# Two-layer attention encoder: the norms between the layers and the transposed rows, ScalarE and VectorE put in the order in which they are written

## The chip, the cores and the metric

The kernel runs on one core of one Trainium2 chip. The metric is the device time of one execution in microseconds (us), less is better. A trace holds one execution as the hardware profiler saw it; its span runs from the first instruction to the last, and the time of that execution is a little longer.

## What is computed

A token sequence of 512 rows of width 1024 goes through two layers in float32. Layer A is latent attention, layer B differential attention whose keys and values come from one projection of the residual stream. The part between them is what the change touches:

```
def rmsnorm(x, g):
    y = x * rsqrt(mean(x * x) + EPS)
    return y * g
# end of layer A
o = (o * silu(z)) @ a_w_o
h = x + rmsnorm(o, a_post_g)          # first norm of a token tile
# start of layer B
u  = rmsnorm(h, b_kv_norm_g)          # second norm of a token tile
k, v = split(u @ b_w_kv)              # kb and vb in the kernel
u2 = rmsnorm(h, b_pre_g)              # same norm, other gain
q, z = split(u2 @ b_w_in)             # qb and zb
```

## The kernel before

The 512 tokens are four tiles of 128 rows, called tile 0 to tile 3 here. Every product in float32 is made of three TensorE matmuls over a high and a low part of each operand (`mm3`, lines 186 to 188): for operands w and x these are high·high, then two mixed ones. So each operand is first split: a copy that rounds to the high part (ScalarE by default, line 130, or GpSimd, line 132) and a subtraction that gives the low part (VectorE, line 135).

At the end of layer A, `wo_end` multiplies the gated attention output (`ogh`, `ogl`) by the output weights. Each tile has two halves of 512 columns in PSUM: `st["acc"]` and `st["o1"]`, both called wo in the trace. After a tile's last matmul `done_a(i)` is called. It runs `chain_a(i)`, the two norms of the tile: two squares with a sum on ScalarE (`sq<-wo`), the product with the gain on VectorE (line 633), v (the mean square, line 620), Ln and Exp on ScalarE (lines 304, 305: a first 1/sqrt), a Newton step on VectorE (lines 307 to 309), the new residual rows (`xr`, line 635), and then the same once more for the second norm (`rh`) over `xr`. Last, the first half of the normed rows is written to `hTf` by ScalarE (line 728) and the second half by GpSimd (line 726), which also stores `xr` to DRAM.

These normed rows have their tokens on the partitions. The next products want the tokens along the free dimension, so TensorE transposes them: `trans_h(i)`, eight transposes into two PSUM banks (`hT`). `evac_h(i)` takes them out: a copy on ScalarE (line 747), the product with the gain on VectorE (`hg`, line 749), and the split into `hT1h` (ScalarE) and `hT1l` (VectorE). Within `done_a(2)` TensorE transposes tile 0, within `done_a(3)` tile 1; tiles 2 and 3 are transposed in `vb_half0`, behind the products vb of tile 0 and of tile 1.

`vb_half0` makes the first half of layer B's values, one tile after the other (vb, 24 matmuls each: four pairs of contraction blocks, of which blocks 0 to 3 need the first half of `hT1h` and `hT1l` of that tile, blocks 4 to 7 the second half). Each is taken out by a split into `vhb` and `vlb`. Behind it the units of the key projection follow, kb, each 24 matmuls with a weight of its own.

The weights come through a stream of units: a load into one of two buffers `wr`, the split into one of three `wh` and three `wl` (or `sp`), and `ws.ahead()` splits up to two units ahead. The last line of `vb_half0` is such a call: it splits the weights of kb units 0 and 1, on ScalarE and VectorE.

What runs in which order: TensorE's instructions stand in program order inside these blocks (`pe_order`). The other engines' instructions are put in order by a scheduler at build time, which goes by its own estimate of when each is ready.

Of the kernel before, what the change touches and what calls it, by code (L numbers as in the profile page):

```python
# [15 lines left out]
AF = mybir.ActivationFunctionType  # L16
ALU = mybir.AluOpType
# [9 lines left out]
EPS = 1e-6  # L27
# [30 lines left out]
def f(ap):  # L58
    return ap.bitcast(F32)


class Stream:
# [32 lines left out]
    def split(self, upto):  # L95
        self.load(upto)
        while self.n_split < min(upto, len(self.units)):
            k = self.n_split
            to = [self.units[k][1](n, k) for n in range(2)]
            if to[0] is None:  # L100
                return
            raw = self.raw.pop(k)
            kc, m = raw.shape[1], raw.shape[2]
            if k in self.tailed:
                hi, lo = (t[:, None, :m + 64] for t in to)
                self.nc.vector.tensor_copy(hi[:, :, :m], raw)
                for a, o in ((0, lo[:, :, :m - 64]), (m - 64, hi[:, :, m:])):
                    v = slice(a, a + o.shape[2])
                    self.nc.vector.tensor_tensor(o, raw[:, :, v], f(hi[:, :, v]), op=ALU.subtract)
            else:  # L110
                hi, lo = (t[:, :kc * m].rearrange("p (k m) -> p k m", k=kc) for t in to)
                split(self.nc, hi, lo, raw, *(self.units[k][2] or self.eng))
            self.done[k] = (hi, lo)
            self.n_split += 1
# [23 lines left out]
def body(tc, ins, outs, dbg=None):  # L138
    nc = tc.nc
    ctx = ExitStack()  # L140
    with ctx:
        _body(ctx, tc, nc, ins, outs, dbg or {})


def _body(ctx, tc, nc, ins, out, dbg):
# [14 lines left out]
    act, dve, gps, pe = nc.scalar, nc.vector, nc.gpsimd, nc.tensor  # L160

    def ps(name):
        return psp.tile([P, 512], F32, tag="ps", name=name)

    def big_t(name, dt=F32R):
        return big.tile([P, 8, 512], dt, tag="big", name=name)

    def hd_t(name, dt=F32R):
        return hd.tile([P, 512], dt, tag="hd", name=name)

    def tmp_t(name, dt=F32):
        return tmp.tile([P, 512], dt, tag="tmp", name=name)
# [4 lines left out]
    def sm_t(name, n=4, bufs=None):  # L177
        return sm.tile([P, n], F32, tag=name, name=name, bufs=bufs)
# [5 lines left out]
    def mm3(o, w, x, first, last):  # L184

        pe.matmul(o, w[0], x[0], start=first, stop=False)  # L186
        pe.matmul(o, w[0], x[1], start=False, stop=False)  # L187
        pe.matmul(o, w[1], x[0], start=False, stop=last)  # L188
# [114 lines left out]
    def rsqrt_cols(r, v2, n):  # L303
        act.activation(r, v2, AF.Ln, scale=2.0)
        act.activation(r, r, AF.Exp, scale=-0.5)
        t = sm_t(f"nt{n}", n)
        dve.tensor_tensor(t, r, r, op=ALU.mult)
        dve.tensor_tensor(t, t, v2, op=ALU.mult)
        dve.scalar_tensor_tensor(r, t, 1.5, r, op0=ALU.subtract, op1=ALU.mult, reverse0=True)
# [32 lines left out]
    for kc in range(KC):  # L342
        for c in first if kc == 0 else [slice(0, 512)]:
            behind = act.activation(xh[:, kc, c], xr[:, kc, c], AF.Copy, scale=col(C_PRE + kc))
        dve.scalar_tensor_tensor(xl[:, kc], xr[:, kc], col(C_PRE + kc), f(xh[:, kc]),
                                 op0=ALU.mult, op1=ALU.subtract)
        g = [ws.get()]
# [3 lines left out]
        sq = acc_x if kc == 0 else hd_t("sqx", F32)  # L351
# [56 lines left out]
    for m in range(4):  # L408
        sq = acc_kv if m == 0 else hd_t("sqkv", F32)
# [23 lines left out]
    for m in range(4):  # L433
        t = tmp_t("cn")
# [38 lines left out]
    for n in range(2):  # L473
        o = [ps(f"va{n}_{i}") for i in range(NT)]
# [127 lines left out]
    def rows(src, name, new=lambda n: hd_t(n, F32)):  # L602
        t = [new(name + "0"), new(name + "1")]
        for n in range(2):
            nc.sync.dma_start(t[n], src[n])
        return t

    def bcast_row(src, name):
        return rows([bass.AP(src.tensor, src.offset + 512 * n, [[0, P], [1, 512]]) for n in range(2)], name, tab_t)

    half_mean = math.sqrt(0.5 / D)

    def inv_norm(r, halves, junk):
        ss, v2 = sm_t("ss", 3), sm_t("v2", 1)
        for n, o in enumerate(halves):
            act.activation(junk[n], o, AF.Square, scale=half_mean, accum_out=ss[:, n:n + 1])
        for n in range(2, len(halves)):
            dve.tensor_tensor(ss[:, 0:1], ss[:, 0:1], ss[:, n - 1:n], op=ALU.add)
        n = len(halves) - 1
        dve.scalar_tensor_tensor(v2, ss[:, 0:1], 0.5 * EPS, ss[:, n:n + 1], op0=ALU.add, op1=ALU.add)  # L620
        rsqrt_cols(r, v2, 1)

    v3 = lambda a: a.rearrange("p (k t) -> p k t", k=4)

    def j3(a, like):
        return v3(a) if len(like.shape) == 3 else a[:, :like.shape[1]]

    def post(parts, done=None):

        r = sm_t("r", 1)  # L630
        inv_norm(r, [o for o, _, _, _ in parts], [j3(tmp_t("sq"), o) for o, _, _, _ in parts])
        for o, g, _, t in parts:
            dve.tensor_tensor(t, o, g, op=ALU.mult)
        for n, (_, _, res, t) in enumerate(parts):
            dve.scalar_tensor_tensor(res, t, r, res, op0=ALU.mult, op1=ALU.add)
            if done:
                done(n)

    st = {}
# [10 lines left out]
    pe_order = lambda: tc.manual_schedule(engines={mybir.EngineType.PE})  # L650
# [64 lines left out]
    hrows = {}  # L715

    def chain_a(i, o1):
        res = xrows[i]
        ts = [hTf[:, 4 * n:4 * n + 4, i * P:i * P + P] for n in range(2)]
        post([(v3(o), v3(g), v3(x), t) for o, g, x, t in zip((st["acc"][i], o1), g_a, res, ts)])  # L720
        r = sm_t("rh", 1)
        inv_norm(r, [v3(a) for a in res], ts)
        for n in range(2):
            gps.dma_start(hdr[i, n], res[n])
            if n:
                gps.tensor_scalar(ts[n], v3(res[n]), r, 1.0, op0=ALU.mult, op1=ALU.mult)
            else:
                act.activation(ts[n], v3(res[n]), AF.Copy, scale=r)
        hrows[i] = ts

    gkv_b = cols[:, C_BKV:C_BKV + 8]

# [2 lines left out]
    def trans_h(i):  # L735
        hh = hrows.pop(i)
        hps[i] = [ps(f"hT{i}_{n}") for n in range(2)]
        for n, o in enumerate(hps[i]):
            for j in range(4):
                pe.transpose(o[:, j * P:j * P + P], hh[n][:, j], ident)  # L740

    def evac_h(i):
        ti = slice(i * P, i * P + P)
        for n, o in enumerate(hps.pop(i)):
            ov = o.rearrange("p (k t) -> p k t", k=4)
            ks = slice(4 * n, 4 * n + 4)
            act.activation(hTf[:, ks, ti], ov, AF.Copy)
            t = tmp_t("hg").rearrange("p (k t) -> p k t", k=4)
            dve.tensor_tensor(t, ov, gkv_b[:, ks].unsqueeze(2).to_broadcast([P, 4, P]), op=ALU.mult)
            split(nc, hT1h[:, ks, ti], hT1l[:, ks, ti], t)  # L750

    vb = {}

    def v_evac(i, n, o):
        split(nc, vb["h"][:, 2 * i + n], vb["l"][:, 2 * i + n], o)

    def vb_half0():
        vb["h"], vb["l"] = big_t("vhb"), big_t("vlb")
        for i in range(NT):
            ti = slice(i * P, i * P + P)  # L760
            o = ps(f"vb0_{i}")
            for kc in range(KC):
                w = wv[kc // 2]
                mm3(o, (hT1h[:, kc, ti], hT1l[:, kc, ti]), (w[0][:, kc % 2], w[1][:, kc % 2]), kc == 0, kc == KC - 1)
            v_evac(i, 0, o)
            if i < 2:
                trans_h(i + 2)
                evac_h(i + 2)
        ws.ahead()

    wv = []
# [1 line left out]
    def done_a(i):  # L773
        if i == 0:
            w1.clear()
        if i > 1:
            trans_h(i - 2)
        chain_a(i, st["o1", i])
        if i > 1:
            evac_h(i - 2)  # L780
        wv.append(ws.get())
        if i < 2:
            ws.ahead()

    g_a = bcast_row(ins["a_post_g"], "ga")
    xrows = [rows([ins["x"][i, n] for n in range(2)], f"xr{i}") for i in range(NT)]
    with pe_order():
        wo_end(lambda h: None, done_a)
        vb_half0()
    vh, vl = vb["h"], vb["l"]  # L790
# [77 lines left out]
    def unit(nm, m):  # L868

        x = (hT1h, hT1l) if nm == "k" else (hT2h, hT2l)  # L870
        w = ws.get()
        o = ps(f"{nm}b{m}")
        for kc in range(KC):
            if kc == KC // 2:
                yield
            mm3(o, (w[0][:, kc], w[1][:, kc]), (x[0][:, kc], x[1][:, kc]), kc == 0, kc == KC - 1)
        ws.ahead()
        evac(nm, m, o)
        yield

    halves = (None for nm, m in beside for _ in unit(nm, m))
# [102 lines left out]
    with pe_order():  # L984
        for nm, m in dense:
            for kc in (2 * m, 2 * m + 1) if nm == "k" else ():
# [3 lines left out]
                                         op0=ALU.mult, op1=ALU.subtract)  # L990
# [108 lines left out]
```

## Time and profile before

| | us |
|---|---|
| median of 3 runs | 579.29 (578.07 to 579.3) |
| the profiled execution, its own time | 577.81 |
| its span | 576.0 |
| TensorE (matmuls) busy | 566.2 |
| VectorE busy | 371.0 |
| ScalarE busy | 282.5 |
| GpSimd busy | 126.0 |

Busy matmul time is a modelled share, since matmuls overlap. What counts is whether TensorE stands still between two matmuls, and for whom.

### The profile page before, as it was taken

How to read it: one execution, taken by the hardware profiler on the slowest of the kernel's cores; microseconds unless marked ns; L12 is line 12 of the kernel's file. 1: busy time of each engine (PE TensorE's matmuls, PEld its weight loads, DVE VectorE, ACT ScalarE, POOL GpSimd, SP SyncE). 2: the span in 40 equal slices, each digit the busy share in tenths (PEclk: the TensorE clock that was granted, in tenths of full speed). 3: DMA queues.
4: the chain of work that ended last, by engine and by line, in shares of the span. 5: the costliest groups of instructions: out<-in, count | busy, mean ns of one | idle time of the engine just before them, and what ended most of it. 6: DMA issues, size and time to landing. Idle time of an engine off the chain costs nothing.

```text
span 576.0 us, 7766 instructions
## 1 busy us (share of the span) xinstructions
PE 566.2 (98%) x2749; PEld 477.5 (83%) x2749; DVE 371.0 (64%) x728; ACT 282.5 (49%) x598; POOL 126.0 (22%) x153
## 2 busy tenths in 40 slices
PE   8999999999999999999999999999999999999995
PEld 7888888888888888888887888888888888888785
DVE  6859855246586666865676575436666767687554
ACT  6157364344455454421475330115674696986432
POOL 1032300000131213333211233222213222234000
PEclk9999999999999999999999999999999999999998
DMA  8342343312322113355331267845745735557012
GB/s 295 114 140 74 110 129 109 101 54 69 102 60 65 55 49 108 129 192 181 121 110 47 73 177 235 271 154 187 247 158 190 247 118 182 185 170 261 1 57 91
DMA packets 32135, 78.00 MB, mean 135 GB/s; under 512 B 3792, under 2 KB 4448, under 8 KB 32096
## 3 DMA queue, kind: packets, MB, share of 16 engines
q1 hardware_dynamic: 26048, 57.16, 30.1%
q0 software_dynamic: 5424, 19.42, 11.0%
q10 hardware_dynamic: 624, 0.92, 0.6%
q8 instruction: 22, 0.36, 0.2%
q14 instruction: 17, 0.14, 0.1%
HBM read 64.11 MB, written 12.58 MB: 133 GB/s over the span
## 4 chain that ended last, share of the span: by engine, by line
PE 90%; DMA 4%; DVE 3%; issue 1%; ACT 1%; POOL 1%; SPq 0%; DVEq 0%; POOLq 0%
PE wo L188 4%; PE wo L186 4%; PE wo L187 4%; PE za L186 3%; PE zb L186 3%; PE zb L187 3%; PE kb L186 3%; PE vb L188 3%; PE qb L188 3%; PE kb L188 3%; PE vb L186 3%; PE qb L186 3%; PE za L188 3%; PE kb L187 3%; PE qb L187 3%; PE za L187 3%
## 5 line engine op out<-in xcount | busy, mean ns | idle before, releaser
L135 DVE TENSOR_TENSOR wl<-wr,wh 128x1024 fp32r<-128x1024 f32 (+2 forms) x76 | 90.6, 1192 | 49.7 <-ACT wh L130 28.0
L132 POOL TENSOR_SCALAR wh<-wr 128x1024 fp32r<-128x1024 f32 x36 | 40.7, 1132 | 104.4 <-PE zb L187 26.7
L130 ACT ACTIVATE wh<-wr 128x1024 fp32r<-128x1024 f32 (+2 forms) x38 | 34.2, 900 | 49.9 <-PE za L187 15.3
L553 POOL TENSOR_SCALAR ea<-ea,ria 128x128 f32<-128x128 f32 (+3 forms) x32 | 18.9, 610 | 71.4 <-DVE ria L530 71.4
L135 DVE TENSOR_TENSOR ptl<-pt,pth 128x512 fp32r<-128x512 f32 (+1 forms) x48 | 26.2, 593 | 4.7 <-ACT pth L130 4.5
L525 ACT ACTIVATE ea<-ea,mxa 128x128 f32<-128x128 f32 (+3 forms) x32 | 18.0, 563 | 21.8 <-DVE mxa L522 21.5
L130 ACT ACTIVATE pth<-pt 128x512 fp32r<-128x512 f32 (+1 forms) x48 | 22.0, 525 | 12.4 <-PE pt L565 12.4
L186 PE MATMUL wo<-w1h,ogh 128*128 128x512 f32 (+1 forms) x72 | 26.8, 372 | 0.0
L188 PE MATMUL wo<-w1h,ogl 128*128 128x512 f32 (+1 forms) x72 | 26.5, 368 | 0.0
L187 PE MATMUL wo<-w1l,ogh 128*128 128x512 f32 (+1 forms) x72 | 26.4, 366 | 0.0
L186 PE MATMUL wo<-wh,ogh 128*128 128x512 f32 x64 | 25.3, 396 | 0.0
L188 PE MATMUL wo<-wh,ogl 128*128 128x512 f32 x64 | 25.1, 392 | 0.2 <-DVE ogl L135 0.2
L186 PE MATMUL zb<-hT2h,wh 128*128 128x512 f32 x64 | 25.3, 395 | 0.0
L186 PE MATMUL kb<-hT1h,wh 128*128 128x512 f32 x64 | 25.1, 393 | 0.0
L186 PE MATMUL za<-xh,wh 128*128 128x512 f32 x64 | 25.0, 391 | 0.0
L186 PE MATMUL qb<-hT2h,wh 128*128 128x512 f32 x64 | 25.0, 391 | 0.0
L188 PE MATMUL zb<-hT2h,wl 128*128 128x512 f32 x64 | 25.0, 391 | 0.0
L187 PE MATMUL zb<-hT2l,wh 128*128 128x512 f32 x64 | 25.0, 390 | 0.0
L187 PE MATMUL wo<-wl,ogh 128*128 128x512 f32 x64 | 25.0, 390 | 0.0
L188 PE MATMUL qb<-hT2h,wl 128*128 128x512 f32 x64 | 24.9, 390 | 0.0
L187 PE MATMUL kb<-hT1l,wh 128*128 128x512 f32 x64 | 24.9, 390 | 0.0
L188 PE MATMUL kb<-hT1h,wl 128*128 128x512 f32 x64 | 24.9, 390 | 0.0
(336 smaller groups left out, 1687.4 us busy)
## 6 DMA issues: line engine op xcount, KB each, us to landing
wr<-in_w_za SPq DMA_DIRECT2D x8, 512.0 KB, 3.6
wr<-in_w_oa SPq DMA_DIRECT2D x8, 512.0 KB, 3.6
wr<-in_w_qb POOLq DMA_DIRECT2D x8, 512.0 KB, 4.6
kh<-kdr SPq DMA_DIRECT2D x16, 256.0 KB, 4.1
kl<-kdr SPq DMA_DIRECT2D x16, 256.0 KB, 4.1
q<-qdr SPq DMA_DIRECT2D x16, 256.0 KB, 3.8
wr<-in_w_zb POOLq DMA_DIRECT2D x8, 512.0 KB, 3.9
wr<-in_w_ob POOLq DMA_DIRECT2D x8, 512.0 KB, 5.0
```

The lines of the kernel that those rows point to most:

```text
L130: nc.scalar.activation(hi, src, AF.Copy)
L132: nc.gpsimd.tensor_scalar(hi, src, 1.0, 1.0, op0=ALU.mult, op1=ALU.mult)
L135: (nc.vector if lo_eng == "dve" else nc.gpsimd).tensor_tensor(lo, src, f(hi), op=ALU.subtract)
L186: pe.matmul(o, w[0], x[0], start=first, stop=False)
L187: pe.matmul(o, w[0], x[1], start=False, stop=False)
L188: pe.matmul(o, w[1], x[0], start=False, stop=last)
L525: act.activation(ev, ev, AF.Exp, bias=mx[:, one], scale=-1.0, accum_out=l[:, one])
L553: gps.tensor_scalar(ev, ev, ri[:, i:i + 1], 1.0, op0=ALU.mult, op1=ALU.mult)
```

## The change

ScalarE and VectorE join TensorE in following the program's order over `wo_end` and `vb_half0`. The program is rewritten so that this order interleaves the work by hand: `chain_a(i)` is cut into four pieces by `yield`, and `evac_h(i - 2)` into three. `done_a(i)` runs one piece of the tile's norms, then one piece of the evacuation of the tile two before it, and so on. In `vb_half0` the evacuation of tiles 2 and 3 runs in one go behind the take-out of vb. The Newton step has two instructions in place of three, both products with the gain stand ahead of v, and both copies out of the transposes stand ahead of the first split. GpSimd and the DMA queues are left to the scheduler.

```
     def chain_a(i, o1):
...
-        post([(v3(o), v3(g), v3(x), t) for o, g, x, t in zip((st["acc"][i], o1), g_a, res, ts)])
-        r = sm_t("rh", 1)
-        inv_norm(r, [v3(a) for a in res], ts)
+        parts = list(zip((st["acc"][i], o1), g_a, res, ts))
+        r, rh = sm_t("r", 1), sm_t("rh", 1)
+        ss, v2 = sums([v3(o) for o, _, _, _ in parts], [v3(tmp_t("sq")) for _ in parts])
+        for o, g, _, t in parts:
+            dve.tensor_tensor(t, v3(o), v3(g), op=ALU.mult)
+        total(ss, v2)
+        guess(r, v2)
+        yield
+        newton(r, v2)
+        for n, (_, _, x, t) in enumerate(parts):
+            dve.scalar_tensor_tensor(v3(x), t, r, v3(x), op0=ALU.mult, op1=ALU.add)
+        yield
+        ss, v2 = sums([v3(x) for x in res], ts)
+        total(ss, v2)
+        guess(rh, v2)
+        yield
+        newton(rh, v2)
         for n in range(2):
             gps.dma_start(hdr[i, n], res[n])
             if n:
-                gps.tensor_scalar(ts[n], v3(res[n]), r, 1.0, op0=ALU.mult, op1=ALU.mult)
+                gps.tensor_scalar(ts[n], v3(res[n]), rh, 1.0, op0=ALU.mult, op1=ALU.mult)
             else:
-                act.activation(ts[n], v3(res[n]), AF.Copy, scale=r)
+                act.activation(ts[n], v3(res[n]), AF.Copy, scale=rh)
         hrows[i] = ts
+        yield
+
+    def sums(halves, junk):
+        ss, v2 = sm_t("ss", 3), sm_t("v2", 1)
+        for n, o in enumerate(halves):
+            act.activation(junk[n], o, AF.Square, scale=half_mean, accum_out=ss[:, n:n + 1])
+        return ss, v2
+
+    def total(ss, v2):
+        dve.scalar_tensor_tensor(v2, ss[:, 0:1], 0.5 * EPS, ss[:, 1:2], op0=ALU.add, op1=ALU.add)
+
+    def guess(r, v2):
+        act.activation(r, v2, AF.Ln, scale=2.0)
+        act.activation(r, r, AF.Exp, scale=-0.5)
+
+    def newton(r, v2):
+        t = sm_t("nt1", 1)
+        dve.scalar_tensor_tensor(t, r, r, v2, op0=ALU.mult, op1=ALU.mult)
+        dve.scalar_tensor_tensor(r, t, 1.5, r, op0=ALU.subtract, op1=ALU.mult, reverse0=True)
...
     def evac_h(i):
+
         ti = slice(i * P, i * P + P)
+        halves = []
         for n, o in enumerate(hps.pop(i)):
...
             dve.tensor_tensor(t, ov, gkv_b[:, ks].unsqueeze(2).to_broadcast([P, 4, P]), op=ALU.mult)
+            halves.append((ks, t))
+        for ks, t in halves:
+            yield
             split(nc, hT1h[:, ks, ti], hT1l[:, ks, ti], t)
+        yield
...
                 trans_h(i + 2)
-                evac_h(i + 2)
+                for _ in evac_h(i + 2):
+                    pass
         ws.ahead()
...
-        chain_a(i, st["o1", i])
-        if i > 1:
-            evac_h(i - 2)
+        evac = evac_h(i - 2) if i > 1 else iter(())
+        for _ in chain_a(i, st["o1", i]):
+            next(evac, None)
         wv.append(ws.get())
...
-    with pe_order():
+    with tc.manual_schedule(engines={mybir.EngineType.PE, mybir.EngineType.Activation, mybir.EngineType.DVE}):
         wo_end(lambda h: None, done_a)
         vb_half0()
```

What stands where now, at three places.

ScalarE at the norms of tile 3, before. Names: `wo_3` are tile 3's two PSUM halves, `xr_2412` and `xr_2413` tile 2's residual rows, `hT_0_2690` and `hT_1_2691` the transposed rows of tile 1:

```order
L616 ACTIVATE hTf,ss<-xr_2412 128x4x128
L616 ACTIVATE sq,ss<-wo_3_2213 128x512
L616 ACTIVATE sq,ss<-wo_3_2665 128x512
L747 ACTIVATE hTf<-hT_0_2690 128x4x128
L747 ACTIVATE hTf<-hT_1_2691 128x4x128
L616 ACTIVATE hTf,ss<-xr_2413 128x4x128
L130 ACTIVATE hT1h<-hg 128x4x128 x2
L304 ACTIVATE rh<-v_2638 128x1
L304 ACTIVATE r<-v_2704 128x1
```

The same place now (`xr_2412` is tile 2's, `xr_2416` and `xr_2417` are tile 3's, `hT_0_2684` and `hT_1_2685` tile 1's transposed rows):

```order
L743 ACTIVATE hTf<-xr_2412,rh 128x4x128
L750 ACTIVATE sq,ss<-wo_3_2213 128x512
L750 ACTIVATE sq,ss<-wo_3_2659 128x512
L757 ACTIVATE r<-v_2699 128x1
L758 ACTIVATE r<-r 128x1
L783 ACTIVATE hTf<-hT_0_2684 128x4x128
L783 ACTIVATE hTf<-hT_1_2685 128x4x128
L130 ACTIVATE hT1h<-hg 128x4x128
L750 ACTIVATE hTf,ss<-xr_2416 128x4x128
L750 ACTIVATE hTf,ss<-xr_2417 128x4x128
```

Tile 3's first square stood among tile 2's second norm; it now stands behind the last instruction of tile 2, and tile 1's transposed rows behind tile 3's Ln and Exp.

VectorE at the same tile, before (`hT1l` is the low part of tile 1's transposed rows):

```order
L633 TENSOR_TENSOR hTf<-wo_3_2213,ga_2400 128x4x128
L633 TENSOR_TENSOR hTf<-wo_3_2665,ga_2401 128x4x128
L749 TENSOR_TENSOR hg<-hT_0_2690,cols 128x512
L749 TENSOR_TENSOR hg<-hT_1_2691,cols 128x512
L620 SCALAR_TENSOR_TENSOR v_2638<-ss 128x1
L620 SCALAR_TENSOR_TENSOR v_2704<-ss 128x1
L135 TENSOR_TENSOR hT1l<-hg,hT1h 128x4x128 x2
L307 TENSOR_TENSOR nt_2644<-rh 128x1
```

And now:

```order
L725 TENSOR_TENSOR hTf<-wo_3_2659,ga_2401 128x4x128
L754 SCALAR_TENSOR_TENSOR v_2699<-ss 128x1
L785 TENSOR_TENSOR hg<-hT_0_2684,cols 128x512
L785 TENSOR_TENSOR hg<-hT_1_2685,cols 128x512
L762 SCALAR_TENSOR_TENSOR nt_2713<-r,v_2699 128x1
L763 SCALAR_TENSOR_TENSOR r<-nt_2713,r 128x1
L731 SCALAR_TENSOR_TENSOR xr_2416<-hTf,r,xr_2416 128x512
L731 SCALAR_TENSOR_TENSOR xr_2417<-hTf,r,xr_2417 128x512
L135 TENSOR_TENSOR hT1l<-hg,hT1h 128x4x128
L754 SCALAR_TENSOR_TENSOR v_2721<-ss 128x1
L135 TENSOR_TENSOR hT1l<-hg,hT1h 128x4x128
L762 SCALAR_TENSOR_TENSOR nt_2729<-rh,v_2721 128x1
```

The low part of tile 1 followed its products with the gain at once; it now stands behind both of tile 3's new residual rows, its second half behind tile 3's second v as well.

ScalarE at the weight copy of kb unit 0, before (`wh_2898`):

```order
L747 ACTIVATE hTf<-hT_0_2608 128x4x128
L728 ACTIVATE hTf<-xr_2408,rh 128x4x128
L304 ACTIVATE r<-v_2622 128x1
L747 ACTIVATE hTf<-hT_1_2609 128x4x128
L130 ACTIVATE wh_2898<-wr_2574 128x1024
L305 ACTIVATE r<-r 128x1
```

And now (`wh_2890`; vb_3 is vb of tile 3):

```order
L1029 ACTIVATE hT2h<-hTf,cols 128x512 x4
L130 ACTIVATE vhb<-vb_2_2832 128x512
L130 ACTIVATE vhb<-vb_3_2859 128x512
L130 ACTIVATE wh_2890<-wr_2570 128x1024
L130 ACTIVATE wh_2894<-wr_2886 128x1024
L130 ACTIVATE ksh<-ra 128x512 x2
```

The copy stood among tile 2's first norm and tile 0's transposed rows; it now stands behind the take-out of the last vb product. On VectorE its subtraction (`wl`) likewise stands behind `vlb` of tile 3. On TensorE one row moves: the first matmul of kb unit 0 stood inside vb of tile 3 and now follows it.

## Rows read from the trace of the kernel before

**Rows 1.** The page, busy time: us, share of the span, count.

```profile
PE 566.2 (98%) x2749; PEld 477.5 (83%) x2749; DVE 371.0 (64%) x728; ACT 282.5 (49%) x598; POOL 126.0 (22%) x153
```

**Rows 2.** Waits in 300 to 325 us, TensorE: us in total, times, longest.

```profile
PE hT L740 <- ACT hTf L728: 1.3, 1, 1.3
```

**Rows 3.** Timeline of TensorE: start us, us, instruction, idle before and releaser.

```profile
297.80 0.47 PE L186 MATMUL vb<-wh,hT1h 128*128 128x512 f32 x1
...
303.12 0.39 PE L188 MATMUL vb<-sp,hT1l 128*128 128x512 f32 x1
304.81 1.10 PE L740 MATMUL hT<-ident,hTf 128*128 128x128 f32 x8 [1.30 <-ACT hTf L728]
305.66 0.48 PE L186 MATMUL vb<-wh,hT1h 128*128 128x512 f32 x1
...
318.01 0.39 PE L186 MATMUL kb<-hT1h,wh 128*128 128x512 f32 x1
...
323.23 0.39 PE L187 MATMUL kb<-hT1l,wh 128*128 128x512 f32 x1
323.45 0.39 PE L188 MATMUL kb<-hT1h,wl 128*128 128x512 f32 x1
```

**Rows 4.** Timeline of ScalarE, the norms of tile 0 (and one square of tile 1).

```profile
277.27 0.60 ACT L616 ACTIVATE sq<-wo 128x512 f32<-128x512 f32 x1 [4.86 <-PE wo L188]
...
278.01 0.60 ACT L616 ACTIVATE sq<-wo 128x512 f32<-128x512 f32 x1
278.50 0.19 ACT L616 ACTIVATION_READ_ACCUMULATOR sq<-wo 128x1 f32 x1
278.92 0.20 ACT L304 ACTIVATE r<-v 128x1 f32<-128x1 f32 x1 [0.23 <-DVE v L620]
279.16 0.20 ACT L305 ACTIVATE r<-r 128x1 f32<-128x1 f32 x1
280.76 0.63 ACT L616 ACTIVATE hTf<-xr 128x512 f32<-128x512 f32 x1 [1.40 <-DVE xr L635]
...
281.39 0.58 ACT L616 ACTIVATE sq<-wo 128x512 f32<-128x512 f32 x1
```

**Rows 5.** Timeline of VectorE, the first norm of tile 0.

```profile
277.99 0.69 DVE L633 TENSOR_TENSOR hTf<-wo,ga 128x512 f32<-128x512 f32 x1 [0.56 <-ACT sq L616]
278.73 0.16 DVE L620 SCALAR_TENSOR_TENSOR v<-ss 128x1 f32<-128x1 f32 x1
...
279.40 0.15 DVE L307 TENSOR_TENSOR nt<-r 128x1 f32<-128x1 f32 x1
...
279.98 1.42 DVE L635 SCALAR_TENSOR_TENSOR xr<-hTf,r,xr 128x512 f32<-128x512 f32 x2
```

**Rows 6.** Timeline of ScalarE, tile 1's normed rows and the weight copy.

```profile
291.25 0.72 ACT L728 ACTIVATE hTf<-xr,rh 128x512 f32<-128x512 f32 x1
...
292.44 1.07 ACT L130 ACTIVATE wh<-wr 128x1024 fp32r<-128x1024 f32 x1
293.39 0.20 ACT L305 ACTIVATE r<-r 128x1 f32<-128x1 f32 x1
```

**Rows 7.** Timeline of VectorE at the same place.

```profile
293.54 1.23 DVE L135 TENSOR_TENSOR wl<-wr,wh 128x1024 fp32r<-128x1024 f32 x1 [0.26 <-ACT wh L130]
294.68 0.15 DVE L307 TENSOR_TENSOR nt<-r 128x1 f32<-128x1 f32 x1
294.75 1.28 DVE L135 TENSOR_TENSOR hT1l<-hg,hT1h 128x512 fp32r<-128x512 f32 x2
```

**Rows 8.** Timeline of ScalarE, take-outs of vb and the copy of kb unit 1's weight.

```profile
319.21 0.57 ACT L130 ACTIVATE vhb<-vb 128x512 fp32r<-128x512 f32 x1
319.69 1.05 ACT L130 ACTIVATE wh<-wr 128x1024 fp32r<-128x1024 f32 x1
323.43 0.60 ACT L130 ACTIVATE vhb<-vb 128x512 fp32r<-128x512 f32 x1 [2.69 <-PE vb L188]
```

**Rows 9.** Busy time in 304 to 311 us; the eighth figure is TensorE's granted clock.

```profile
304.00:311.00 7.00, 6.19 (x32) 5.27 (x33) 4.57 (x11) 5.14 (x13) 2.11 (x3) 1.00 0.20 75
```

## The prediction

> **What bounds the kernel now.** I read the busy shares first, then TensorE's waits, then the timelines of the three engines around the place. TensorE is busy for 98% of the span [rows 1]: any time it gains or loses comes out at the end. Between 300 and 325 us it has one wait only, 1.3 us at the transposes of tile 2, for ScalarE's normed rows of that tile [rows 2]. In the timeline the last matmul of vb of tile 0 starts at 303.12 and the transposes start at 304.81; matmuls follow each other 0.227 us apart (323.23 to 323.45, rounded), so the transposes could have started at 303.35 and the slot lost is 1.46 us [rows 3]. That is all that a better order of the two helpers can return.
>
> Why were those rows late? ScalarE had begun tile 2's Ln when it took up the weight copy of kb unit 0 at 292.44, and tile 2's Exp came behind it at 293.39 [rows 6]. VectorE then did the subtraction of the same weight at 293.54, and tile 2's Newton step came at 294.68 although its Exp had ended at 293.59 [rows 6, 7]. A weight that TensorE first uses at 318.01 [rows 3] stood in the way of rows it wanted at 303.35.
>
> **The change, step by step.** All three orders are fixed now, so I walk through them with the durations of before.
>
> *One tile's norms alone.* On ScalarE the distance from a tile's first square to the next tile's first square is now a chain that nothing overlaps:
> - two squares: the second starts 0.63 behind the first (280.76 to 281.39), and its sum is read 0.68 after its start (278.01 to 278.50 and 0.19): 1.31 [rows 4].
> - the second product with the gain now stands ahead of v, and a product out of PSUM starts only when ScalarE has read that bank (0.56 idle, released by the square): 0.04 hand-off, 0.69, and v 0.16 less an overlap of 0.07: 0.82 [rows 5]. Before, v needed 0.20 here.
> - Ln and Exp: from v's end at 278.89 to Exp's end at 279.36, 0.47 [rows 4, 5].
> - Newton: before, three small instructions took 0.58 (279.40 to 279.98), 0.19 each; now two, 0.39, and 0.04 of hand-off: 0.43 [rows 5].
> - two residual updates, 1.42 [rows 5]; then the second square of them, 0.07 after and 0.68 long: 2.17 [rows 4].
> - v, Ln, Exp and Newton again: 0.20, 0.47, 0.39.
> - the normed rows: 0.04 and 0.72, and ScalarE's next instruction starts 0.1 before their end (as Exp at 293.39 before the copy's end at 293.51): 0.66 [rows 6]. The GpSimd half runs beside it.
>
> The sum is 6.9; with the rounding of the hand-offs I take 7.0. Two thirds of it is waiting: ScalarE holds the next tile's squares behind it, which before ran inside the gap (a square of tile 1 at 281.39 [rows 4]).
>
> *With an evacuation interleaved.* Two copies out of the transposes and two products stand between Exp and Newton. The copies follow each other by 0.48 (as 319.21 and 319.69 [rows 8]), each 0.6; the products are 0.69 [rows 5], start 0.04 behind a copy, the second in the pipeline of the first. Newton starts 1.7 later. After the second Exp, the copy and the subtraction of the second half (0.60 [rows 8] and 0.64 [rows 7], less overlaps) push the second Newton by 1.1. So 9.8 for tiles 2 and 3. Within such a block the first half of the evacuated tile's low part is done 6.8 after the block's start (behind both residual updates), its second half 8.9 after.
>
> *The clock of ScalarE.* Tile 0 starts at 277.27 and waits 0.1 for its second half [rows 4]: it ends at 284.3. Tile 1 ends at 291.3, tile 2 at 301.1, tile 3 at 310.9. The two `sp` subtractions that move behind tile 0 and tile 1 on VectorE cost 1.2 each and fit into the time in which ScalarE squares the next tile (1.3): nothing. If that cover is gone, a few tenths are added.
>
> *What TensorE sees.*
> 1. vb of tile 0 at 297.80 wants tile 0's low part 0.5 later [rows 3]. It is ready at 291.3 + 6.8 = 298.1, the second half at 300.2, and wanted at about 301.0: nothing, to 0.1.
> 2. Transposes of tile 2 at 303.35: its rows are ready at 301.2. The wait is gone: −1.46.
> 3. vb of tile 1 could start 0.85 later (304.81 to 305.66 [rows 3]), at 304.2. Its high part is written in tile 3's block, 4.5 after its start: 301.1 + 4.5 = 305.6. Wait 1.45. Two matmuls go, the third wants the low part: 301.1 + 6.8 = 307.9, plus the hand-off 308.0, against 306.15. Wait 1.85. The second half is ready at 310.0, wanted at 310.7.
> 4. Tiles 2 and 3 are evacuated behind tile 3's block without norms between, and arrive within 0.1 of the time wanted: nothing.
> 5. kb unit 0: its weight copy waits behind the take-out of vb of tile 3. The take-out starts one hand-off, 0.04, behind the last matmul; the copy follows 0.48 later (319.21 to 319.69 [rows 8]) and takes 1.07 [rows 6]. vb's last matmul (0.39) ends 0.16 after the next one could start, so the high part is there 0.16 + 0.04 + 0.48 + 1.07 + 0.04 = 1.8 late. The subtraction takes 1.23 [rows 7]; the two matmuls that need only the high part cover 0.45 of it: another 0.8. Wait 2.6. What queues behind: kb unit 1's copy and subtraction, which end within 2.3 us more while unit 0 has 5 to go, and the load of unit 2, which waits for unit 0's raw buffer and is wanted two units, 10.9 us, later: nothing.
>
> The matmul of kb unit 0 that stood at 318.01 inside vb [rows 3] only changes place. The sum is 1.45 + 1.85 + 2.6 − 1.46 = **+4.4**. Against the profiled execution's own time (577.81) that is 582.2, against the median of the three runs, 1.5 above it, **583.7**.
>
> *Bounds.* The hand-offs are the least certain: some 14 in a block of norms, of 0.04 each, and three blocks lie ahead of the late low part. At nothing each they take 1.5 off, at twice the size they add 1.5: +2.9 to +5.9. I keep the middle, since the rows of before show 0.03 to 0.07 with few exceptions.
>
> *A rule weighed.* That Newton came behind the weight's subtraction though its input was there 1.1 us before [rows 6, 7] shows VectorE taking its instructions strictly in turn. The Trainium skill says the same of the helpers (PSUM — Partial Sum Buffer, Engine vs sequencer instructions: their queues are strictly first in, first out); by it the weight copy cannot pass, which is step 5. If an instruction with its inputs ready could pass a waiting one, the 2.6 of step 5 and most of step 3 would vanish and the sum would be that of the rival that is faster.
>
> **The rivals.**
> - *Only one of the two waits.* If the norms run faster than I add up, so that tile 1's low part is there by 304.7 (306.15 less the 1.45 of the first wait; 3.2 us earlier than I reckon, more than the hand-offs hold), steps 1 to 4 leave −1.46, and step 5 stays: +1.1, 580.4. For it: VectorE is busy for only 4.57 of the 7 us from 304 to 311 [rows 9]. Against: the chain is of latencies, not of busy time. Chance 0.07. The other way round, step 3 without step 5 (if the weight were there after all): +1.8, 581.1, chance 0.04; the order speaks against it.
> - *Faster.* The wait of 1.46 goes and nothing takes its place: 577.8. It needs tile 1's low part 3.2 us earlier and the copy of kb unit 0 anywhere ahead of the last take-out; from either missing on, it is not faster. Chance 0.05.
> - *TensorE's clock.* The waits of step 3 come as 1.45 and 1.9 within 2.5 us. Through the 1.3 us wait of before the granted clock stayed at 1.00, the level of 2.4 GHz, in 304 to 311 [rows 9], and the matmul behind it was as long as others. If it fell to 1.2 GHz behind the longer ones, each matmul would take twice its 0.23; over the 22 remaining matmuls of vb of tile 1 that is 5 us more, 588.7. The Trainium skill (TensorE: Matmul & The Clock Gate, What's actually happening) says that the throttled state is the default and activity releases it; no row here shows TensorE working at the lower level. Chance 0.06.
>
> **How the numbers follow.** Forecast 0.76; the rivals 0.07, 0.04, 0.05, 0.06; 0.02 for what I don't see. The range takes in the bounds of the hand-offs (582.2 to 585.2), the 1.5 by which single runs differ, and the rival at 581.1: 581.0 to 586.3; it leaves out about 0.18. A difference of 0.2% (1.2 us) is about what a measurement of this kernel can tell from none. Faster by more 0.05; within it 0.06, mostly the rival at +1.1; slower 0.89.
>
> **What would show it.** In the profile after: no wait of TensorE for the normed rows of tile 2; two new waits at vb of tile 1, the first for ScalarE's `hT1h`, the second for VectorE's `hT1l`, some 3.3 together; two at kb's first matmuls, for ScalarE's `wh` and VectorE's `wl`, some 2.6 together. On ScalarE the first squares of tiles 1, 2 and 3 at about 284.3, 291.3 and 301.1. The forecast is wrong if tile 3's square starts before 299, or if the weight copy stands ahead of the last `vhb`.

## The result, and the profile after

The changed kernel takes 586.51 us (median of 4 runs, 586.39 to 586.87) against 579.29 before. The ratio is given as 1.015, 95% interval 1.0129 to 1.017. The quotient of the two medians is 1.0125, a little under that interval; the times of the runs do not show why, so the argument below rests on the traces. The kernel is slower, as forecast, and 0.2 us above the forecast's range: 583.7 us was predicted, 586.3 at most.

The page after, busy time, to be read beside [rows 1]:

```profile
PE 571.5 (98%) x2749; PEld 481.1 (82%) x2749; DVE 370.6 (63%) x720; ACT 283.8 (49%) x598; POOL 127.2 (22%) x153
```

The number of matmuls is the same, yet TensorE is busy 5.3 us longer. A wait adds little to busy time (it undoes the overlap of two matmuls, 0.39 us long and 0.23 apart), so most of this says that some matmuls took longer.

TensorE's waits after, all of the execution (us in total, times, longest), to be read beside [rows 2]:

```profile
PE kb L186 <- ACT wh L130: 1.6, 1, 1.6
PE vb L188 <- DVE hT1l L135: 1.6, 1, 1.6
PE vb L186 <- ACT hT1h L130: 1.3, 1, 1.3
PE warm L287 <- DVE ones L275: 1.0, 1, 1.0
PE kb L188 <- DVE wl L135: 0.5, 1, 0.5
PE g L362 <- ACT xh L344: 0.3, 1, 0.3
```

The wait for tile 2's normed rows is gone. The four waits that were predicted are there (the rows of vb and kb), at the instructions and for the releasers that were named.

ScalarE's timeline after (start us, us, instruction, idle before and releaser): the first square of tiles 1, 2 and 3, and the end of the stretch. In [rows 4] a square of tile 1 stood at 281.39, among tile 0's norms.

```profile
284.48 0.58 ACT L750 ACTIVATE sq<-wo 128x512 f32<-128x512 f32 x1
...
291.44 0.58 ACT L750 ACTIVATE sq<-wo 128x512 f32<-128x512 f32 x1
...
301.28 0.58 ACT L750 ACTIVATE sq<-wo 128x512 f32<-128x512 f32 x1
...
327.95 0.60 ACT L130 ACTIVATE vhb<-vb 128x512 fp32r<-128x512 f32 x1 [3.40 <-PE vb L188]
328.45 2.00 ACT L130 ACTIVATE wh<-wr 128x1024 fp32r<-128x1024 f32 x2
```

A block of norms takes 6.96 us alone (284.48 to 291.44) and 9.84 with an evacuation inside (to 301.28); 7.0 and 9.8 were worked out. The copies of kb's weights follow the last take-out, with ScalarE idle for 3.40 us ahead of it.

TensorE's timeline after, to be read beside [rows 3]:

```profile
303.44 1.03 PE L774 MATMUL hT<-ident,hTf 128*128 128x128 f32 x8
305.73 0.50 PE L186 MATMUL vb<-wh,hT1h 128*128 128x512 f32 x1 [1.25 <-ACT hT1h L130]
306.07 0.40 PE L187 MATMUL vb<-wl,hT1h 128*128 128x512 f32 x1
308.05 0.80 PE L188 MATMUL vb<-wh,hT1l 128*128 128x512 f32 x1 [1.58 <-DVE hT1l L135]
308.64 0.63 PE L186 MATMUL vb<-wh,hT1h 128*128 128x512 f32 x1
309.06 0.63 PE L187 MATMUL vb<-wl,hT1h 128*128 128x512 f32 x1
...
313.33 0.63 PE L188 MATMUL vb<-sp,hT1l 128*128 128x512 f32 x1
313.76 0.55 PE L186 MATMUL vb<-sp,hT1h 128*128 128x512 f32 x1
314.14 0.39 PE L187 MATMUL vb<-sp,hT1h 128*128 128x512 f32 x1
...
315.98 1.03 PE L774 MATMUL hT<-ident,hTf 128*128 128x128 f32 x8
```

Behind the second wait each matmul is 0.63 us long and the next one follows 0.43 later, where it was 0.39 and 0.23. The busy times of that stretch and of the one behind kb's waits show why (the eighth figure is the granted clock), beside [rows 9]:

```profile
304.00:311.00 7.00, 4.17 (x14) 2.94 (x13) 4.73 (x11) 4.24 (x11) 1.50 (x3) 0.73 0.20 75
311.00:318.00 7.00, 7.00 (x29) 5.72 (x29) 4.37 (x7) 4.48 (x9) 0.31 (x1) 0.78 0.01 4
318.00:325.00 7.00, 7.00 (x32) 5.82 (x31) 5.64 (x15) 4.37 (x8) 0.00 (x0) 1.00 0.07 19
325.00:332.00 7.00, 4.84 (x18) 3.32 (x18) 3.67 (x5) 2.49 (x3) 0.00 (x0) 0.94 0.01 4
332.00:339.00 7.00, 7.00 (x27) 5.65 (x26) 2.26 (x3) 0.00 (x0) 3.26 (x4) 0.82 0.55 159
```

For part of these stretches TensorE ran at the lower of its two levels, 1.2 in place of 2.4 GHz; before, all of them stood at 1.00.

**One measure for all kernels.** Executions differ by up to 3.3 us in what lies ahead of this place (its start lies between 296.4 and 299.7 us in the ten profiles), with no link to the edits: the two profiles of the change have it at 297.1 and 298.9. The difference arises at the very start. From 7 to 9 us TensorE works on 10 or 11 matmuls in four of the profiles and on 6 in the other six, and in those six this place comes at 298.5 or later. So I compare one stretch: from the start of tile 1's transposes to the start of kb unit 0's 12th matmul. Before it is 28.48 us (297.01 to 325.49), after 37.46 (297.10 to 334.56): +8.98. The span grew by 8.5.

The sum of that stretch. Waits as time lost between two matmuls, which includes the pipelining that a wait undoes: 305.73 against 304.23, where the first matmul could have started (0.79 behind the transposes, as 297.10 to 297.89 one tile earlier), 1.50; 308.05 against 306.30, 1.75; at kb 329.55 against 327.76 and 330.81 against 330.12, 1.79 and 0.69. Together 5.73, less the 1.46 that went: +4.27, where +4.4 was predicted. The lower clock: from 308.05 to 315.98 stand 22 matmuls, 7.93 us. Behind a wait but at a clock of 1.00, the same 22 take 5.12 in run c3 below (307.90 to 313.02). From 330.81 to 334.56 stand nine, 3.75 us, against 2.18 in run c0 below (331.36 to 333.54): together +4.38. That matmuls start more slowly behind a wait, at either clock, is another 0.27 (at 0.227 each the 22 take 4.99 and the nine 2.04). The three make 8.92 of the 8.98.

### The profile page after: what moved, and what is told of

It is laid out like the page before. It is cut to its first block, busy times and chain, and to the rows that moved or that the text cites. A ratio compares the mean times of both kernels' runs of the same rounds, so it can differ in the third digit from the quotient of the medians.

```text
span 584.5 us, 7761 instructions
## 1 busy us (share of the span) xinstructions
PE 571.5 (98%) x2749; PEld 481.1 (82%) x2749; DVE 370.6 (63%) x720; ACT 283.8 (49%) x598; POOL 127.2 (22%) x153
## 4 chain that ended last, share of the span: by engine, by line
PE 89%; DVE 5%; ACT 3%; DMA 1%; issue 1%; POOL 0%; DVEq 0%; POOLq 0%; ACTq 0%
PE wo L188 4%; PE wo L186 4%; PE wo L187 4%; PE pt L565 3%; PE kb L188 3%; PE kb L186 3%; PE kb L187 3%; PE za L186 3%; PE zb L186 3%; PE zb L188 2%; PE zb L187 2%; PE qb L187 2%; PE qb L186 2%; PE qb L188 2%; PE za L188 2%; PE za L187 2%
```

## The experiments

Theory A: two separate waits, one for tile 1's transposed rows behind a chain of norms, one for kb's weight behind the last take-out, and after each a stretch at the lower clock because TensorE stood still. Against it: the weight alone, or the interleaving, or the fixed order as such. All runs compute the whole result.

| kernel | stretch, us | over before | TensorE's waits in it | matmuls of 0.63 us | ratio to before (95%) |
|---|---|---|---|---|---|
| before | 28.48 | | 1.30 | 0 | |
| the change | 37.46 | +8.98 | 1.25, 1.58, 1.63, 0.53 | 19 | 1.015 (1.0129 to 1.017) |
| c0, the change again | 34.67 | +6.19 | 1.25, 1.58, 1.63, 0.53 | 7 | 1.0092 (1.0071 to 1.0112) |
| a1, weight early | 31.84 | +3.36 | 1.25, 1.58 | 6 | 1.0052 (1.0032 to 1.0072) |
| a2, TensorE kept at work | 33.36 | +4.88 | none | 0 | 1.0103 (1.0077 to 1.0128) |
| b1, before with the weight held back | 26.95 | −1.53 | none | 0 | 0.9968 (0.9952 to 0.9984) |
| b2, before in fixed order | 43.84 | +15.36 | 4.60, 3.43, 1.63, 0.53 | 22 | 1.0244 (1.0216 to 1.0272) |
| c1, weight early, rows first | 29.83 | +1.35 | 0.75, 1.37 | 0 | 1.0019 (1.0004 to 1.0035) |
| c3, weight early, v first | 28.72 | +0.24 | 1.38 | 0 | 0.9989 (0.9974 to 1.0005) |
| c4, weight early, kept at work | 30.45 | +1.97 | none | 0 | 1.0026 (1.0012 to 1.0039) |

The stretch is from one profile each. The ratio is from timed runs, each beside the kernel before on the same chip: a1, a2, b1 and b2 on one chip, c0 to c4 on another.

**a1: kb's weight early.** One line in `vb_half0`, behind the evacuation of tile 3:

```
                 for _ in evac_h(i + 2):
                     pass
+            if i == 1:
+                ws.split(ws.n_get + 1)
```

> The changed kernel with one thing undone: kb unit 0's weight is split right behind tile 3's transposed rows, ahead of the take-outs of vb of tiles 2 and 3, and no longer behind the last of them. Theory A (two separate waits of TensorE, each followed by a stretch at the lower clock): the two waits at kb (1.6 and 0.5 us) go, and the eight matmuls that follow them 0.43 us apart run 0.23 apart; from vb's last matmul to kb's first use of the low part 2.6 us less, behind it 1.25 us less: about 3.9 us faster than the change, 582.7 us. The waits at vb of tile 1 stay at 1.3 and 1.6 us. Rival B (the weight copy is the whole loss and the interleaving is sound): all 7.2 us come back and the wait that went stays away, 578 to 579 us. Rival C (the loss is in vb of tile 1 alone): under 1 us.

TensorE's waits of a1, from 297 us on only these two (the two rows hold for the whole execution):

```profile
PE vb L188 <- DVE hT1l L135: 1.6, 1, 1.6
PE vb L186 <- ACT hT1h L130: 1.2, 1, 1.2
```

Its busy times behind those two waits (the eighth figure is the clock):

```profile
304.00:311.00 7.00, 4.18 (x19) 3.01 (x19) 5.04 (x11) 4.53 (x14) 1.13 (x2) 0.92 0.10 37
311.00:318.00 7.00, 7.00 (x32) 5.77 (x31) 4.70 (x9) 4.86 (x10) 0.69 (x1) 0.84 0.11 41
```

Both waits at kb are gone and the two at vb stay as they were, so those at kb came from the place of the weight copy in the order. The stretch is 5.6 us shorter than in the change's first profile, not 3.9: this execution also left the lower clock sooner behind the first pair (6 matmuls of 0.63 in place of 12). Against c0's profile it is 2.8 shorter. Rival B is out, since 3.4 us remain, and so is rival C.

**a2: TensorE kept at work.** The added matmuls are overwritten or never read:

```
             o = ps(f"vb0_{i}")
+            for _ in range(14 if i == 1 else 0):
+                pe.matmul(o, hT1h[:, 0, 0:P], wv[2][0][:, 0], start=True, stop=True)
...
+        idle = ps("idle")
+        for _ in range(11):
+            pe.matmul(idle, hT1h[:, 0, 0:P], wv[2][0][:, 0], start=True, stop=True)
         ws.ahead()
```

> The changed kernel with 25 matmuls added that nobody reads: 14 ahead of vb of tile 1 (into its own PSUM bank, overwritten by its first matmul) and 11 ahead of kb, so that TensorE works through the time in which it waited. Theory A (the clock falls because TensorE stands still): granted clock 1.00 throughout, matmuls 0.23 us apart behind both places; vb of tile 1 ends 2.9 us earlier and kb's start 1.25 us earlier although work was added: 582.3 us. Rival (the clock falls there for another reason, or the waits alone make the loss): no faster than the change, 586.5 us, or slower by what the added matmuls outlast the waits.

TensorE's timeline of a2 at vb of tile 1, and its busy times there (the eighth figure is the clock):

```profile
306.36 3.43 PE L803 MATMUL vb<-sp,hT1h 128*128 128x512 f32 x14
309.63 0.39 PE L186 MATMUL vb<-wh,hT1h 128*128 128x512 f32 x1
309.86 0.39 PE L187 MATMUL vb<-wl,hT1h 128*128 128x512 f32 x1
310.29 0.50 PE L188 MATMUL vb<-wh,hT1l 128*128 128x512 f32 x1
310.63 0.40 PE L186 MATMUL vb<-wh,hT1h 128*128 128x512 f32 x1
```

```profile
304.00:311.00 7.00, 6.96 (x35) 5.56 (x34) 5.11 (x11) 4.53 (x16) 1.13 (x2) 1.00 0.08 33
311.00:318.00 7.00, 7.00 (x37) 5.72 (x36) 4.90 (x10) 5.45 (x11) 0.69 (x1) 1.00 0.15 51
```

The low part comes no sooner, TensorE only no longer stands still for it, and the clock stays at 1.00. With 25 matmuls more the stretch is 4.1 us shorter than in the change's first profile (4.2 expected) and 1.3 shorter than in c0. That the standing still causes the low clock is shown by this, and by the timed executions: the mean granted clock is 0.998 or 0.999 in all four of a2, 0.988 to 0.994 in all eight of the change (c0 among them), and 0.996 to 0.999 in those of before. The time itself missed: 582.3 would be 0.5% over before, and 1.0% was measured, less than the change's first 1.5% but no less than c0's 0.92%.

**b1: the weight held back in the kernel before.** Here the scheduler's order is kept; `split` and `v_evac` return the ScalarE copy, and one edge is added:

```
-            v_evac(i, 0, o)
+            out = v_evac(i, 0, o)
+            if i == 1:
+                anchor = out
...
-        ws.ahead()
+        with tc.issue_after(anchor.ins):
+            ws.ahead()
```

> The kernel before, scheduler's order on ScalarE and VectorE, with one edge added: kb units 0 and 1's weight copies may not be issued ahead of the take-out of vb of tile 1. Theory A (the wait of before came from that weight copy standing in tile 2's norms, and nothing else): TensorE's 1.3 us wait at the transposes of tile 2 goes and no other comes, about 1.4 us faster than before, 577.8 us. Rival (the norms of tile 2 are late anyway, the weight copy only fills a gap): the wait stays over 0.8 us and the time within 0.5 us of before.

TensorE's timeline of b1 where [rows 3] has its wait of 1.30:

```profile
303.14 0.39 PE L190 MATMUL vb<-sp,hT1l 128*128 128x512 f32 x1
303.38 1.03 PE L742 MATMUL hT<-ident,hTf 128*128 128x128 f32 x8
304.17 0.48 PE L188 MATMUL vb<-wh,hT1h 128*128 128x512 f32 x1
```

No wait is left from 297 us to kb, and the stretch is 1.53 us shorter. So the weight, copied and subtracted in the middle of tile 2's norms [rows 6, 7], was the whole cause of the wait that the change set out from. It is the fastest kernel here, faster than before by 0.32% (0.16 to 0.48).

**b2: the fixed order without interleaving.** The kernel before with the change's last line alone:

```
-    with pe_order():
+    with tc.manual_schedule(engines={mybir.EngineType.PE, mybir.EngineType.Activation, mybir.EngineType.DVE}):
         wo_end(lambda h: None, done_a)
         vb_half0()
```

> The kernel before with its program as it was (no interleaving by hand) and only the engines' order fixed to program order: a tile's norms whole, then the evacuation of the tile two before it. Theory A (a fixed order makes the norms a chain of some 7 us per tile in which nothing overlaps, and what stands behind it waits): waits of about 3 us at vb of tile 0 and again at vb of tile 1, and the two at kb; with the lower clock behind each, 590 to 596 us: slower than the change. Rival C (the interleaving by hand is what costs, the fixed order does not): faster than the change, 580 to 584 us.

TensorE's waits of b2:

```profile
PE vb L186 <- ACT hT1h L130: 8.0, 2, 4.6
PE kb L186 <- ACT wh L130: 1.6, 1, 1.6
...
PE kb L188 <- DVE wl L135: 0.5, 1, 0.5
```

The waits at vb of tiles 0 and 1 are 4.60 and 3.43, longer than the 3 that I expected, and the time is within what was expected. Behind each of the two, single as they are, the clock fell (6 and 11 matmuls of 0.63). So the loss comes with the fixed order of the program as it was, and rival C is out. What the change adds to that order (the interleaving, but also the shorter Newton step and the place of the products) gives back two fifths of the stretch's loss, three fifths by c0; the runs do not separate these. Nor is a fixed order slow as such: c3 below keeps it and takes the time of before.

**c0: the change again.** 

> The changed kernel again, beside the kernel before on this chip, so that the others of this group have it as their measure. 7 to 8.5 us over before. The same two pairs of waits; how many matmuls behind each pair run 0.43 us apart may differ from the first profile (13 and 8 there), which would be where its times scatter.

The four waits are the same to 0.05 us, but only 7 matmuls stand at 0.63 behind the first pair and none behind the second. The ratio is lower than the first one and its interval does not reach it, so my expectation of 7 us and more missed (0.92% is 5.3 us). Busy times of c0 behind kb's waits:

```profile
325.00:332.00 7.00, 4.84 (x21) 3.39 (x20) 3.95 (x6) 2.77 (x4) 0.00 (x0) 1.00 0.00 0
332.00:339.00 7.00, 7.00 (x33) 5.77 (x32) 2.27 (x3) 0.00 (x0) 3.05 (x4) 1.00 0.44 154
```

Behind the first pair c0's clock did fall:

```profile
304.00:311.00 7.00, 4.18 (x20) 2.98 (x19) 4.84 (x11) 4.52 (x14) 1.13 (x2) 0.94 0.13 48
311.00:318.00 7.00, 7.00 (x31) 5.77 (x30) 4.81 (x10) 4.77 (x10) 0.68 (x1) 0.82 0.08 30
```

What the waits cost, with the slower start behind them and less the wait that went, is the same in both profiles, 4.6 us; what the clock adds was 4.4 in the first and 1.6 in this one (6.73 for the 22 matmuls, against 5.12).

**c1: the rows first.** As a1, and in `done_a`:

```
-        evac = evac_h(i - 2) if i > 1 else iter(())
-        for _ in chain_a(i, st["o1", i]):
-            next(evac, None)
+        for _ in evac_h(i - 2) if i > 1 else ():
+            pass
+        for _ in chain_a(i, st["o1", i]):
+            pass
```

> The changed kernel with kb's weight early (as a1_weight_early) and the interleaving undone the other way: the transposed rows of the tile two back are taken out whole ahead of a tile's norms. Theory A (each block of norms is a chain, and what stands behind a block is late by the block's length): tile 1's rows come in time for vb of tile 1, so no wait there; instead the normed rows of tile 3 are some 1.6 us late for their transposes and tile 2's rows another 1.6 us late for vb of tile 2; with the tile 2 wait gone 2.0 us over before if the clock holds, up to 3 us more if it falls behind either. Rival C (the interleaving is what costs): no wait over 0.5 us, 1 us faster than before.

TensorE's waits of c1 in the stretch:

```profile
PE vb L186 <- ACT hT1h L130: 1.4, 1, 1.4
...
PE hT L774 <- ACT hTf L743: 0.8, 1, 0.8
```

They moved to the two places named, tile 3's normed rows (0.75) and vb of tile 2 (1.37), the first at half its expected size, and the stretch is 1.35 us over before where 2.0 was expected. Nothing waits at vb of tile 1 any more: what is late is what stands behind a block of norms. The clock held at 1.00.

**c3: v first.** As a1, and in `chain_a`:

```
-        for o, g, _, t in parts:
-            dve.tensor_tensor(t, v3(o), v3(g), op=ALU.mult)
-        total(ss, v2)
+        for n, (o, g, _, t) in enumerate(parts):
+            if n:
+                total(ss, v2)
+            dve.tensor_tensor(t, v3(o), v3(g), op=ALU.mult)
```

> The changed kernel with kb's weight early, and the second product with the gain put behind v again, as in the kernel before: one instruction per tile moved on VectorE. Theory A (the block of a tile's norms is a chain, 7.0 and 9.8 us; each term in it counts once per tile): the block is 0.62 us shorter, four times, so the two waits at vb of tile 1 shrink from 1.2 and 1.6 us to none and about 1.2 us (1.5 in time lost), the clock stays at 1.00, and the time is that of before, within 0.7 us. Rival (the waits come from the place of the transposed rows alone): the waits shrink by 0.6 us at most, 2 us or more over before.

ScalarE's timeline of c3, the first squares of tiles 1, 2 and 3, and TensorE's one wait:

```profile
286.12 0.58 ACT L751 ACTIVATE sq<-wo 128x512 f32<-128x512 f32 x1
...
292.48 0.58 ACT L751 ACTIVATE sq<-wo 128x512 f32<-128x512 f32 x1
...
301.73 0.58 ACT L751 ACTIVATE sq<-wo 128x512 f32<-128x512 f32 x1
```

```profile
PE vb L188 <- DVE hT1l L135: 1.4, 1, 1.4
```

Its busy times around that wait:

```profile
304.00:311.00 7.00, 5.62 (x30) 4.41 (x29) 4.74 (x11) 4.24 (x12) 1.65 (x3) 1.00 0.20 75
```

The blocks take 6.36 and 9.25 us, 0.60 and 0.59 less than in the change. One instruction moved per tile took the first wait away and left 1.38 of the second (about 1.2 expected), and the clock stayed at 1.00: the stretch is 3.1 us shorter than a1's. The time is that of before; the mean clock is 0.996 to 0.999 in all twelve timed executions.

**c4: weight early and TensorE kept at work.** a1 with the first part of a2.

> The changed kernel with kb's weight early and 14 matmuls that nobody reads ahead of vb of tile 1. Theory A: no wait of TensorE and granted clock 1.00 from 297 us on; what is left is the time of the added matmuls (3.2 us) and 0.1 to 0.2 behind them less the wait that went (1.46): 1.8 to 2.0 us over before, against 3.0 for a1_weight_early, whose clock fell. Rival (the low clock behind the waits costs nothing of note): equal to a1_weight_early or slower.

Its busy times at vb of tile 1:

```profile
304.00:311.00 7.00, 7.00 (x36) 5.61 (x35) 4.73 (x12) 4.33 (x12) 1.13 (x2) 1.00 0.18 68
```

No wait, clock 1.00, +1.97 us in the stretch, as worked out. The stretch is 1.4 us shorter than a1's although it holds 14 matmuls more; by time, 1.0026 against 1.0052 on another chip, the intervals still touch.

## Why the prediction was wrong

- *What bounds the kernel, and why tile 2's rows were late*: right, shown by b1 (the wait goes with the weight copy, and 1.53 us with it).
- *The blocks of norms*, 7.0 and 9.8 us: 6.96 and 9.84. That a term of such a block counts once per tile is shown by c3 for the one that it moved. Not two thirds of a block is waiting, as was said: ScalarE is busy for 4.08 of the 6.96 us. No term of the sum hangs on this.
- *Steps 1, 2 and 4*: right. No wait at tile 0's vb, none for tile 2's normed rows, none at vb of tiles 2 and 3.
- *Step 3*, 1.45 and 1.85: 1.50 and 1.75. *Step 5*, 2.6: 2.48, and a1 shows that it comes from the weight's place in the order alone. The sum of the waits, +4.4, is +4.27 in the trace.
- *The step that failed* is the rival "TensorE's clock". I argued from one row, that the clock had stayed at 1.00 through the single wait of 1.30 [rows 9], to a chance of 0.06, and so left the term out of the sum. But the change does not make one such wait, it makes two pairs. Behind the first pair (1.25 and 1.58, with two matmuls between) the clock fell in all three profiles that have it, the change's, c0's and a1's; behind the second pair (1.63 and 0.53) in the change's and b2's, not in c0's. In their place a term of its own was due: +4.4 us in the change's profile, 1.6 in c0's. The waits of the sum (+4.4) and the first figure make 8.8 us, and the two profiled executions differ by 8.6. I had also priced the fall for one place only, at 5 us with all 22 matmuls at twice their 0.23. It cost 2.8 there, since 12 of them ran 0.43 apart throughout, and 1.6 more at kb, which I had not priced.
- *How far off the number was is partly chance.* c0's median, 584.07 us, lies inside the forecast's range although the same term was missing.
- *The rule cited there*, that the throttled state is the default and activity releases it (the Trainium skill, TensorE: Matmul & The Clock Gate, What's actually happening), agrees with rows in its second half: in the change's profile the granted clock of 0.73 to 0.82 stands behind standing still, and a2 and c4, in which TensorE has work throughout this stretch, stay at 1.00. That the lower level is the default no run here shows.

What stays open: which pair of waits makes the clock fall in a given execution, and for how long. The runs show the scatter and not its cause. Nor does the clock alone order the times: of the change's four executions the one with the lowest mean clock, 0.988, was the shortest.

## What to carry to other kernels

A fixed order on a helper engine can turn a chain of hand-offs between two engines into a block that nothing overlaps (here 7 us per tile): add up one block with its hand-offs, and ask what stands behind it that the bounding engine wants. Look for calls that end up last in the program text (here the weights of the next stage): under a fixed order they are also last in time. When a sum shows the matmul engine standing still twice in short order, price the lower clock behind it as a term, with a wide bound, and try the smallest edge on the scheduler's own order first (b1) before replacing that order.

## What was unexpected of the hardware

Adding matmuls shortened the stretch: with 25 that nobody reads it is 4.1 us shorter than in one profile of the change and 1.3 shorter than in the other. By time that is a gain over the change's first ratio (1.0103 against 1.015) and none over c0's (1.0092). The cost of the same waits was not the same twice: 19 matmuls of 0.63 us in one profile, 7 in the next. Single or more loosely spaced waits of much the same length did not lower the clock: 1.30 before, 1.38 in c3, and 0.75 and 1.37 in c1 with the eight transposes between. Longer single ones did, 4.60 and 3.43 in b2.
